# Rows of x and first value weights moved from a hand-written order into the planner's streams, with square sums of the first outputs ranked last

## Chip, cores and metric

The kernel runs on one core of one Trainium2 chip. The metric is the device time of one execution in microseconds (us). The engines are named as in the profile: PE is TensorE, ACT ScalarE, DVE VectorE, POOL GpSimd, SP SyncE, which issues every DMA.

## Reference

One layer of a streaming encoder with 1024 rows of 1024 float32 values. What concerns the change is its beginning and the end of its attention:

```python
h = rmsnorm(x, g_mix_pre)
proj = h @ w_in                   # fq fk fv f_logit cq ck cv
y_fox = forgetting_attention(fq, fk, fv, f_logit)         # 8 heads of 64, causal
y_chk = chunked_relpos_attention(cq, ck, cv, rel_bias)    # 8 heads of 64, 9 chunks
y = concat(rmsnorm(y_fox, g_fox_out), rmsnorm(y_chk, g_chk_out))
x = x + rmsnorm(y @ w_out, g_mix_post)
```

Then follow a cross-attention into 256 memory tokens (`w_mq`, `w_mk`, `w_mv`, `w_mo`) and a squared-ReLU MLP with 4096 hidden values, each with its norms and its residual.

## The kernel before

**Products.** Every float32 product is made of three matmuls (`mm3`, L191 to L195). Each operand is split into a rounded copy, hi, made by ACT, and a difference, lo, made by DVE or POOL as operand minus hi; hi x hi, hi x lo and lo x hi are summed in a PSUM bank. So nothing can be multiplied before ACT has written its hi and DVE or POOL its lo. The PSUM has two banks under each of four names, `mm`, `s`, `tr` and `pv`.

**First part, written out by hand** (L1345 to L1397). The 1024 rows of x are eight blocks x0 to x7 of 128 rows. For each block, `load_x` (L263) issues the load, `norm_x` (L269) takes the sum of squares on ACT (L208), the inverse root on POOL in two operations on 128x1 (L202, L203) and the scaling by root and gain, `gpre`, on DVE (L272). `to_T` (L211) turns two blocks at a time with 16 PE transposes (L218) into the `tr` and `s` banks; ACT copies each bank to `hT_hi` (L231) and DVE subtracts for `hT_lo` (L232). `gpre` is the gain spread over 128 partitions by a PE product with ones, copied by DVE (L1356). Two blocks of weights give values for four heads each: `w_v1` in two pieces (four chunks of 128 rows each), `w_v0` in three (three, three and two chunks, with eight gate columns). `value_weights` (L290) loads a piece, `value_split` (L302) and `split_w` (L181) split it: hi on ACT (L187), lo on DVE or POOL (L188). `values` (L311) makes 24 matmuls for one block of rows and one weight, then an ACT copy (L319) and a DVE difference (L322) into the value tile, and a small ACT copy of the gate columns (L321). The order is fixed by a loop over pairs of blocks: values of `w_v1` for the pair, then the transposes of the next pair, then values of `w_v0` for the pair. Three buffers (`wraw`) hold raw weight pieces; a load into one waits until the piece before it has been split. SP issues its DMAs in program order, so what stands behind such a load waits too.

**Attention, ordered by a planner.** `Flow` (L56) is a model run while the kernel is built. Streams (generators such as `score_steps`, `turn_steps`, `value_steps`, `filler_steps`) yield one PE step each with a cost and a condition. The first stream in the list whose condition holds gives the next PE step. Work for ACT, DVE, POOL and SP is put into queues with the time from which it can start, a cost and a rank (`level`); of the work that is due, the lowest rank goes first. `Tokens` count free buffers and banks; `seen` holds when something will be there. The result is a fixed order on each engine; on the chip the engines wait for each other by semaphores. `Stock` (L346) holds the list of weight blocks in the order of loading, splits them and gives the buffers back; `home` names the kind of buffer that each block is split into. `Outputs` (L941) loads the attention outputs back in two head groups and two halves of the rows, and puts the split, the squares and their sum in the queues; `rstd_steps` (L995) sums the squares over partitions on PE. Scores are taken in pieces of two matmuls (L593), reduced by DVE with their bias (L597); probabilities are turned by PE (`ptr`, L671), split by ACT and DVE (`ph` L680, `pl` L677) and multiplied with the values (`pv`, L708 and L709).

Two `flow.run` calls share the work: one for attention, which also makes keys and values of the memory tokens (`mk`, `mv`) as filler, and one for the output projection (`w_out`, tiles `yw`) and the cross-attention. The planner's clock starts at zero where attention starts: it takes all engines for free then. Past the cross-attention, the order is written out by hand again.

## Time and profile before

| what | value |
|---|---|
| median of 3 runs | 1498.51 us (1498.42 to 1498.52) |
| the profiled execution | 1498.03 us |
| its span, first to last instruction | 1496.2 us |
| granted TensorE clock | 0.999 |
| PE busy | 1474.1 us (99%) |
| DVE, ACT, POOL busy | 936.3, 790.3, 402.1 us |

How to read it: the page gives the busy time of each engine, and views of the trace give busy time in stages, the waits of an engine with the instruction that ended them, and single instructions in order of time: start, length, engine, line, operation, out<-in, shape, and in brackets the idle time before it and its releaser. "L188" is a line of the kernel before. A row with "x2" stands for two instructions in a row; rows that summarise give minimum, median and maximum in ns. Records of PE overlap, since matmuls are pipelined: the distance between two starts is what one costs.

### The profile page before, as it was taken

The page shows a single profiled execution, that of the slowest core. Times are in us where ns is not written, and L with a number is a line of the kernel's source. Part 1 is how long each engine was busy: PE and PEld are TensorE (multiplying, and loading weights), DVE is VectorE, ACT ScalarE, POOL GpSimd, SP SyncE. Part 2 cuts the span into 40 slices and gives each one's busy share as a digit, 9 for nine tenths or more (in the row PEclk, how much of TensorE's full clock was granted, in tenths as well). Part 3 has the DMA queues.
Part 4 walks back from the last instruction along what each step waited for, and adds up shares of the span by engine and source line. Part 5 has one row for each costly group of instructions (what it writes and reads, how often), then busy time and mean ns, then how long its engine had stood idle before and what let it go on. Part 6 is the DMA issues. An engine that isn't in the chain of part 4 may idle for free.

```text
span 1496.2 us, 21615 instructions
## 1 busy us (share of the span) xinstructions
PE 1474.1 (99%) x7628; PEld 1253.2 (84%) x7628; DVE 936.3 (63%) x1617; ACT 790.3 (53%) x1405; POOL 402.1 (27%) x629
## 2 busy tenths in 40 slices
PE   8999999999999999999999999999999999999998
PEld 7989888888889888888888887888888888888886
DVE  5377677565576834884375577675555675646577
ACT  5367576575666835554354455555555553444442
POOL 4244355353354300521031423333333000000021
PEclk9999999999999999999999999999999999999999
DMA  4223312512224552461241355774445695436475
GB/s 170 90 74 88 84 40 92 152 53 64 75 67 149 175 176 85 141 211 57 85 169 57 115 180 192 263 244 149 149 151 176 225 346 203 141 120 215 173 252 197
DMA packets 82766, 218.58 MB, mean 146 GB/s; under 512 B 9801, under 2 KB 13905, under 8 KB 82658
## 3 DMA queue, kind: packets, MB, share of 16 engines
q1 hardware_dynamic: 82658, 217.20, 43.7%
q8 instruction: 60, 0.98, 0.3%
q14 instruction: 48, 0.39, 0.1%
HBM read 157.86 MB, written 50.91 MB: 140 GB/s over the span
## 4 chain that ended last, share of the span: by engine, by line
PE 92%; DVE 3%; DMA 1%; POOL 1%; ACT 1%; issue 1%; SPq 0%; DVEq 0%; POOLq 0%; ACTq 0%
PE ptr L671 4%; PE fx L194 4%; PE fx L195 4%; PE fx L193 4%; PE fy L194 3%; PE fy L195 3%; PE fy L193 3%; PE px L195 3%; PE px L194 3%; PE px L193 3%; PE pv L709 2%; PE pv L708 2%; PE k L193 2%; PE k L195 2%; PE k L194 2%; PE pz L193 2%
## 5 line engine op out<-in xcount | busy, mean ns | idle before, releaser
L677 DVE TENSOR_TENSOR pl<-ptr,ph 128x512 fp32r<-128x512 f32 (+1 forms) x152 | 92.2, 615 | 39.7 <-ACT ph L680 33.9
L1788 ACT ACTIVATE whif<-ra 128x1024 fp32r<-128x1024 f32 x37 | 39.2, 1060 | 122.0 <-PE fy L194 62.6
L1790 DVE TENSOR_TENSOR wlof<-ra,whif 128x1024 fp32r<-128x1024 f32 x37 | 45.3, 1224 | 91.1 <-ACT whif L1788 91.1
L680 ACT ACTIVATE ph<-ptr 128x512 fp32r<-128x512 f32 (+1 forms) x152 | 79.2, 539 | 39.2 <-PE ptr L671 32.6
L1904 POOL TENSOR_SCALAR rf<-sf 128x1 f32<-128x1 f32 x8 | 8.2, 1027 | 326.5 <-ACT jf L1889 326.2
L709 PE MATMUL pv<-pl,vs 128*128 128x256 f32 x304 | 78.8, 283 | 1.9 <-DVE pl L677 1.9
L708 PE MATMUL pv<-ph,vs 128*128 128x256 f32 x304 | 79.8, 286 | 0.0
L194 PE MATMUL fx<-vlof,whif 128*128 128x512 f32 x168 | 65.4, 389 | 0.0
L193 PE MATMUL fx<-vhif,whif 128*128 128x512 f32 x168 | 65.4, 389 | 0.0
L195 PE MATMUL fx<-vhif,wlof 128*128 128x512 f32 x168 | 65.4, 389 | 0.0
L709 PEld LDWEIGHTS pv<-pl,vs 128*128 128x128 f32 x304 | 57.6, 189 | 6.7 <-DVE pl L677 1.5
L708 PEld LDWEIGHTS pv<-ph,vs 128*128 128x128 f32 x304 | 57.3, 189 | 4.0
L1678 POOL TENSOR_TENSOR sc<-wf,wf 128x512 f32<-128x512 f32 x14 | 22.0, 1568 | 142.9 <-DMA wf<-in_w_ff 142.9
L193 PE MATMUL k<-hT_hi,whik 128*128 128x512 f32 x128 | 52.7, 412 | 0.0
L193 PE MATMUL mq<-h2T_hi,whimq 128*128 128x512 f32 x128 | 52.1, 407 | 0.0
L193 PE MATMUL q<-hT_hi,whiq 128*128 128x512 f32 x128 | 50.9, 398 | 0.0
L194 PE MATMUL yw<-wlowo,yT_hi 128*128 128x512 f32 x128 | 49.9, 390 | 0.5 <-DVE wlowo L410 0.5
L193 PE MATMUL ym<-whimo,oT_hi 128*128 128x512 f32 x128 | 50.3, 394 | 0.1
L193 PE MATMUL yw<-whiwo,yT_hi 128*128 128x512 f32 x128 | 50.3, 393 | 0.0
L195 PE MATMUL k<-hT_hi,wlok 128*128 128x512 f32 x128 | 50.3, 393 | 0.0
L195 PE MATMUL mq<-h2T_hi,wlomq 128*128 128x512 f32 x128 | 50.1, 392 | 0.0
L195 PE MATMUL q<-hT_hi,wloq 128*128 128x512 f32 x128 | 50.1, 391 | 0.0
(596 smaller groups left out, 5026.1 us busy)
## 6 DMA issues: line engine op xcount, KB each, us to landing
ra<-gd SPq DMA_DIRECT2D x56, 512.0 KB, 4.0
wg<-in_w_ff SPq DMA_DIRECT2D x56, 512.0 KB, 6.0
wf<-in_w_ff SPq DMA_DIRECT2D x38, 512.0 KB, 4.0
gd<-s SPq DMA_DIRECT2D x48, 256.0 KB, 2.1
wrawmq<-in_w_mq SPq DMA_DIRECT2D x16, 512.0 KB, 4.0
wrawmo<-in_w_mo SPq DMA_DIRECT2D x16, 512.0 KB, 3.8
gd<-u SPq DMA_DIRECT2D x32, 256.0 KB, 2.1
gd<-g SPq DMA_DIRECT2D x25, 256.0 KB, 2.5
```

The costliest lines, as they stand in the source:

```text
L193: nc.tensor.matmul(ps, lh, rh, start=start, stop=False, skip_group_check=more)
L194: nc.tensor.matmul(ps, lh, rl, start=False, stop=False, skip_group_check=more)
L195: nc.tensor.matmul(ps, ll, rh, start=False, stop=stop, skip_group_check=more)
L671: nc.tensor.transpose(tr[:, m, :], sp[:, k * P:(k + 1) * P], ident)
L677: flow.put("V", at, 0.7, lambda: nc.vector.tensor_sub(pl[:, live, :], tr[:, live, :], f(ph[:, live, :])), done)
L680: flow.put("S", flow.end, 0.6, lambda ph=ph, tr=tr, live=live: nc.scalar.activation(ph[:, live, :], tr[:, live, :], AF.Copy), split)
L708: nc.tensor.matmul(pv, v, ph[:, hs, :], start=c == 0 and half == 0, stop=False)
L709: nc.tensor.matmul(pv, v, pl[:, hs, :], start=False, stop=c + 1 == len(steps) and half == 1)
L1678: eng.tensor_sub(sc[:, k1], r0[:, k0], r1[:, k0])
L1788: nc.scalar.activation(ah, ra, AF.Copy)
L1790: nc.vector.tensor_sub(al, ra, f(ah))
L1904: nc.gpsimd.tensor_scalar(r, ssf[b][:, 0:1], ssf[b][:, 1:2], EPS, op0=ALU.add, op1=ALU.add)
```

## The change

The hand-written first part is taken out. Loads of x and of the two first value weights become entries of `Stock`'s list (`u1` for `w_v1`, `u0` for `w_v0`), in the order x0, first piece of u1, x1, second piece of u1, x2, first piece of u0, x3, x4, x5, the other two pieces of u0, x6, x7. Two new streams, `x_turn_steps` and `first_value_steps` (once for u1, once for u0), stand ahead of the others in the attention's list, and the planner's clock starts with the first load. x0 and x1 are loaded and squared in two halves of 512 columns; every block is scaled in two halves. x0 to x3 are turned one block at a time, x4 to x7 in pairs. The lo of each piece of u1 is made in halves, one on DVE and one on POOL at the same time; the lo of all pieces of u0 is made by POOL. u1 is split into the `w` buffers as before, u0 into `u4` buffers, both by the planner; the load of the bias row, its reversal and its store (`bias_rows`) become a pump. Scores may begin only once the gates have taken their buffers (`"gating"`). A third piece of `w_mv`'s first half goes to a `u4` buffer. In `Outputs`, all work of the first head group (copies, differences, squares and their sums) gets rank 3, where it had 1. `rstd_steps` for the second half of the first group and the pump of `Outputs` go to the second `flow.run`. The number of matmuls and transposes, and their shapes, stay the same.

```diff
-            dict(s=2, tr=2, pv=2, mm=2, sp=1, p=2, klo=4, bias=2, raw=2, w=0, u4=6,
+            dict(s=2, tr=2, pv=2, mm=2, sp=0, p=2, klo=1, bias=2, raw=3, w=2, u4=6,
...
-            self.blocks = []
+            u = {k: (k, t["w_v0" if k[0] == "u0" else "w_v1"][:, a:b, :], [P, b - a, 264 if k[0] == "u0" else 256])
+                 for k, a, b in ((("u1", 0), 0, 4), (("u1", 1), 4, 8),
+                                 (("u0", 0), 0, 3), (("u0", 1), 3, 6), (("u0", 2), 6, 8))}
+            self.blocks = ["x0", u["u1", 0], "x1", u["u1", 1], "x2", u["u0", 0], "x3", "x4", "x5",
+                           u["u0", 1], u["u0", 2], "x6", "x7", "small"]
+            self.bus = 0.5
...
-            self.home.update({("mv", nh, kp): "u4" for nh in range(2) for kp in (1, 3)})
+            self.home.update({("mv", *k): "u4" for k in ((0, 1), (0, 2), (0, 3), (1, 1), (1, 3))})
             turn = 0
+            self.home.update({("u0", i): "u4" for i in range(3)})
...
+        def moved(self, key, share=1.0):
+
+            def landed(at):
+                self.bus = max(self.bus, at + 1.5) + 1.75 * share
+                seen[key] = self.bus + 0.2
+            flow.put("D", flow.now, 0.42, lambda: None, landed)
...
+                if key[0] == "u1":
+                    both = all_of(key, 2, free["raw"].give)
+
+                    def apart(at, key=key, both=both):
+                        for half, (eng, e, cost) in enumerate((("V", nc.vector, 0.69), ("G", nc.gpsimd, 1.3))):
+                            done = all_of((key, half), 1, both)
+                            flow.put(eng, at, cost, lambda half=half, e=e: self.lo(key, e, half), done)
+
+                    flow.put("S", flow.now, 1.06, lambda key=key: self.hi(key), apart)
+                    continue
+                vec = key[0] not in ("q", "k", "v", "u0") and (key[0] != "mk" or key[1] % 2)
...
+                    if key[0] == "u0":
+                        flow.put(eng, at, 2.1, lambda: self.lo(key, e), last)
...
-                               lambda: there(("qk", n), ("bias", n, a)) and free["s"].ready()
+                               lambda: there(("qk", n), ("bias", n, a), "gating") and free["s"].ready()
...
+            lv = 3 if g == 0 else 1
...
-                flow.chain(at, [("V", 0.7, call) for call in adds], done, 1)
+                flow.chain(at, [("V", 0.7, call) for call in adds], done, lv)
...
-                                dst, o, AF.Square), squared, 1)), 1)
+                                dst, o, AF.Square), squared, lv)), lv)
...
-    def rstd_steps(g):
-
-        for th in range(2):
+    def rstd_steps(g, ths=(0, 1)):
+
+        for th in ths:
...
+    def x_load(b):
+        tag = "sp" if b % 3 else "klo"
+        x = xrow[b] = p1.tile([P, D], F32, tag=tag, bufs=5 if b % 3 else 4, name=f"x_{b}")
+        cols = [slice(0, HT), slice(HT, D)] if b < 2 else [slice(0, D)]
+        r, ss = (small.tile([P, k], F32, tag=m, bufs=8, name=f"{m}_x{b}") for m, k in (("rstd", 1), ("ssx", 2)))
+        def root():
+            if b > 1:
+                nc.gpsimd.tensor_scalar(r, ss[:, 0:1], EPS, None, op0=ALU.add)
+            else:
+                nc.gpsimd.tensor_scalar(r, ss[:, 0:1], ss[:, 1:2], EPS, op0=ALU.add, op1=ALU.add)
+            nc.gpsimd.tensor_tensor(r, r, mhalf[:, 0:1], op=ALU.pow)
+        def scale(h):
+            c = slice(h * HT, (h + 1) * HT)
+            nc.vector.scalar_tensor_tensor(x[:, c], x[:, c], r, gpre[:, c], op0=ALU.mult, op1=ALU.mult)
+        def rooted(at):
+            lv = min(b // 2, 2)
+            flow.put("G", at, 0.95, root, lambda at: flow.chain(at, [("V", 0.7, lambda: scale(0))], lambda at: (
+                mark(("xn", b, 0))(at), flow.put("V", at, 0.7, lambda: scale(1), mark(("xn", b, 1)), lv)), lv))
+        summed = all_of(("ssx", b), len(cols), rooted)
+        for i, c in enumerate(cols):
+            nc.sync.dma_start(x[:, c], t["x"][b * P:(b + 1) * P, c])
+            def square(i=i, c=c):
+                junk = p1.tile([P, D], BF16, tag="ph", bufs=2, name=f"junk{b}{i}")
+                nc.scalar.activation(junk[:, c], x[:, c], AF.Square, scale=1.0 / 32.0, accum_out=ss[:, i:i + 1])
+            def landed(at, square=square):
+                stock.bus = max(stock.bus, at + 1.5) + 1.75 / len(cols)
+                flow.put("S", stock.bus + 0.2, 0.17 + 0.9 / len(cols), square, summed, min(b // 2, 1))
+            flow.put("D", flow.now, 0.42, lambda: None, landed)
...
+    def x_turn_steps():
+        for bs in ((0,), (1,), (2,), (3,), (4, 5), (6, 7)):
+            n = len(bs)
+            act, c0 = hT[bs[0] // 4], bs[0] % 4 * P
+            per = 4 // n
+            for k in range(0, KC, per):
+                bank = ("tr", "s")[k // 4]
+                yield 0.436, lambda: there(*(("xn", b, k // 4) for b in bs)) and free[bank].ready() and (
+                    bs[0] < 2 or ("first", 1, bs[0] - 2) in seen)
+                free[bank].take()
+                tr = mm_tile([P, per, n, P], f"tr_x{bs[0]}_{k}", bank)
+                for j in range(per):
+                    for q, b in enumerate(bs):
+                        nc.tensor.transpose(tr[:, j, q, :], xrow[b][:, (k + j) * P:(k + j + 1) * P], ident)
+                src = tr.rearrange("p a q b -> p a (q b)")
+                left = all_of(("xt", bs, k), per // 2, free[bank].give)
+                for i in range(k // 2, (k + per) // 2):
+                    part = src[:, 2 * i - k:2 * i - k + 2, :]
+                    dh, dl = act.h[i][:, :, c0:c0 + n * P], act.l[i][:, :, c0:c0 + n * P]
+                    def lo(at, part=part, dh=dh, dl=dl, left=left, i=i, bs=bs, n=n):
+                        def there_now(end):
+                            left(end)
+                            for b in bs:
+                                seen["hT", b, i] = end
+                        flow.put("V", at, 0.16 + 0.26 * n, lambda: nc.vector.tensor_sub(dl, part, f(dh)), there_now)
+                    flow.put("S", flow.end, 0.16 + 0.22 * n, lambda part=part, dh=dh: nc.scalar.activation(
+                        dh, part, AF.Copy), lo)
+            for b in bs:
+                free["sp" if b % 3 else "klo"].give(flow.end)
+    def first_value_steps(g):
+        n = 264 if g == 0 else 256
+        blocks = ((0, 3), (3, 6), (6, 8)) if g == 0 else ((0, 4), (4, 8))
+        where = [(i, kc - a) for i, (a, b) in enumerate(blocks) for kc in range(a, b)]
+        def split(at):
+            for pair in (2, 3) if g == 0 else (0, 1):
+                for th in range(2):
+                    seen["v", pair, th] = at
+        done = all_of(("first", g), TB, split)
+        logits = all_of("fcol", TB) if g == 0 else None
+        for kb in range(TB):
+            cs = slice((kb % 4) * P, (kb % 4 + 1) * P)
+            for kc in range(KC):
+                i, j = where[kc]
+                w = ("u0", i) if g == 0 else (("u1", i), j // 2)
+                yield 3 * (n / 2400 + 0.0135), lambda: there(w, ("hT", kb, kc // 2)) and (kc or free["mm"].ready())
+                if kc == 0:
+                    free["mm"].take()
+                    ps = mm_tile([P, n], f"v{g}_{kb}")
+                wh, wl = stock.w[f"u{g}", i]
+                mm3(ps, hT[kb // 4].hi(kc, cs), hT[kb // 4].lo(kc, cs), wh[:, j, :], wl[:, j, :], kc == 0, kc == KC - 1)
+            seen["first", g, kb] = flow.end
+            src = ps[:, 0:256].rearrange("p (h d) -> p h d", d=64)
+            v = vs[g][kb // 2][:, kb % 2, :, :]
+            def lo(at, src=src, v=v):
+                flow.put("V", at, 0.43, lambda: nc.vector.tensor_sub(v[:, :, 64:128], src, f(v[:, :, 0:64])),
+                         lambda end: (free["mm"].give(end), done(end)))
+            def hi(src=src, v=v, ps=ps, kb=kb):
+                nc.scalar.activation(v[:, :, 0:64], src, AF.Copy)
+                if g == 0:
+                    nc.scalar.activation(fcol[:, kb, :], ps[:, 256:264], AF.Copy)
+            flow.put("S", flow.end, 0.38 + 0.1 * (g == 0), hi, lambda at, lo=lo: (logits and logits(at), lo(at)))
+        for i in range(len(blocks)):
+            stock.done((f"u{g}", i))
...
-                seen["v", n, th] = 0.0
-        biases = Biases()
-        flow.pumps += [stock.pump, biases.pump, outputs.pump]
-        flow.run([value_steps(), turn_steps(), score_steps(), side_steps(), rstd_steps(0),
-                  filler_steps(keep)])
+        flow.pumps += [stock.pump, biases.pump, outputs.pump, bias_rows]
+        flow.run([x_turn_steps(), first_value_steps(1), first_value_steps(0), value_steps(), turn_steps(),
+                  score_steps(), side_steps(), rstd_steps(0, (0,)), filler_steps(keep)])
         return keep
 
-    stock = Stock()
+    stock, biases = Stock(), Biases()
+    others = {"norm": (3, mem_norm), "mem": (2, mem_loads), "small": (0, small_loads)}
+    others.update({f"x{b}": (0, lambda b=b: x_load(b)) for b in range(TB)})
...
-        xs = [load_x(0), load_x(1)]
-        raw1 = value_weights(1)
-        xs += [load_x(2), load_x(3)]
...
-        w1 = value_split(1, raw1[0], 0, nc.vector)
-        w1 += value_split(1, raw1[1], 1, nc.gpsimd)
-        to_T(xs[0], xs[1], hT[0], 0, "x0", ("tr", "s"))
-        raw0 = []
-        value_weights(0, raw0, 0)
-        xs += [load_x(4), load_x(5)]
-        value_weights(0, raw0, 1)
-        value_weights(0, raw0, 2)
-        w0 = []
-        for b in range(0, TB, 2):
-            if b + 2 < TB:
-                for i in (b + 2, b + 3):
-                    norm_x(xs[i], i)
-            if b == 0:
-                w0 += value_split(0, raw0[0], 0, nc.vector)
-            values(1, w1, vs[1], b)
-            if b == 0:
-                w0 += value_split(0, raw0[1], 1, nc.gpsimd)
-            values(1, w1, vs[1], b + 1)
-            if b == 0:
-                w0 += value_split(0, raw0[2], 2, nc.gpsimd)
-            if b + 2 < TB:
-                to_T(xs[b + 2], xs[b + 3], hT[(b + 2) // 4], (b // 2 + 1) % 2 * 256, f"x{b + 2}", ("tr", "s"))
-            if b == 0:
-                xs += [load_x(6), load_x(7)]
...
-            if b == 6:
-                stock.split_now(2)
-            for kb in (b, b + 1):
-                values(0, w0, vs[0], kb)
+
+        vs = {g: [u4(f"vs{g}_{i}", (P, 2, 4, P)) for i in range(4)] for g in (1, 0)}
...
-        flow.pumps[1] = Rows().pump
-        flow.run([memory_out_steps(), memory_turn_steps(), memory_score_steps(), rstd_steps(1), second_rows(),
+        flow.pumps[1:] = [Rows().pump, outputs.pump]
+        flow.run([memory_out_steps(), memory_turn_steps(), memory_score_steps(), rstd_steps(0, (1,)), rstd_steps(1), second_rows(),
...
```

164 lines of the change are left out of this document (38 added, 126 removed).

## Prediction

> **What bounds the kernel now.** I read the page first, then busy time by stage, then what TensorE (PE) waited for.
>
> ```profile
> span 1496.2 us, 21615 instructions
> PE 1474.1 (99%) x7628; PEld 1253.2 (84%) x7628; DVE 936.3 (63%) x1617; ACT 790.3 (53%) x1405; POOL 402.1 (27%) x629
> ```
>
> PE is busy for 1474.1 of 1496.2 us, so all idle time together is 22.1 us (1.5%). In the two built programs PE issues the same 7612 matmuls and transposes of the same shapes. The change can therefore only move PE's idle time. Where is it? The first fence is busy time by stage (first number the length, second PE's), the second PE's waits over the whole span (total, times, longest).
>
> ```profile
> 12.17:21.66 9.49, 8.24 (x67) 8.00 (x65) 7.75 (x9) 7.92 (x16) 8.28 (x7) 1.00 0.76 297
> 21.66:65.71 44.05, 44.05 (x368) 44.05 (x369) 18.72 (x33) 15.83 (x39) 10.17 (x13) 1.00 0.13 41
> 100.00:160.00 60.00, 60.00 (x388) 54.15 (x385) 46.22 (x150) 45.27 (x102) 30.29 (x74) 1.00 0.25 68
> 510.00:520.00 10.00, 8.10 (x49) 6.75 (x49) 9.84 (x17) 9.72 (x20) 0.70 (x4) 1.00 0.49 168
> ```
>
> ```profile
> PE tr_x L218 <- DVE x L272: 2.5, 1, 2.5
> PE pv L709 <- DVE pl L677: 1.9, 4, 0.9
> PE v L193 <- DVE vs L322: 1.3, 1, 1.3
> PE yw L194 <- DVE wlowo L410: 0.5, 1, 0.5
> ```
>
> From 21.66 to 65.71, where the first query matmul starts, PE never stops; it does not stop from 100 to 160 either. What the change touches is the start, up to 21.66, and the end of attention at 510 to 520 (1.9 us of waits for the differences pl, 0.5 for a split of w_out). The other waits lie past 550, where PE's order is the same in both programs, so I leave them.
>
> Busy time overstates PE at the start, because a record stretches while PE waits. I count issue distance instead.
>
> ```profile
> 13.34 0.28 PE L195 MATMUL v<-whiv,hT_lo 128*128 128x256 f32 x1
> 13.46 0.28 PE L193 MATMUL v<-whiv,hT_hi 128*128 128x256 f32 x1
> 21.66 0.39 PE L193 MATMUL v<-whiv,hT_hi 128*128 128x264 f32 x1 [1.25 <-DVE vs L322]
> 33.48 1.75 PE tr_x L218 x16
> ```
>
> A value matmul costs 0.12 us (13.34 to 13.46), a transpose 1.75/16 = 0.109. By 21.66 PE had issued 48 value matmuls and 32 transposes: 5.8 + 3.5 = 9.3 us of work, so **12.4 us are idle at the start**. That is the number the change must beat.
>
> **The start.** Removed is the hand-written order; now x and the first value weights are streams of the planner. Half rows are loaded, squared and scaled for x0 and x1; the first weight block is issued ahead of x1; x0 to x3 are turned singly, between value matmuls. Here are the rows that price the steps.
>
> ```profile
> 5.00 1.06 ACT L208 ACTIVATE junk<-x 128x1024 bf16<-128x1024 f32 x1 [3.00 <-DMA x<-in_x]
> 5.96 0.19 ACT L208 ACTIVATION_READ_ACCUMULATOR junk<-x 128x1 f32 x1
> 6.05 0.69 DVE L1356 COPY gpre<-gpre 128x512 f32<-128x512 f32 x1 [1.02 <-PE gpre L1355]
> 6.24 0.23 POOL L202 TENSOR_SCALAR rstd_x<-ss_x 128x1 f32<-128x1 f32 x1 [4.95 <-ACT junk L208]
> 6.55 0.57 POOL L203 TENSOR_TENSOR rstd_x<-rstd_x,mhalf 128x1 f32<-128x1 f32 x1
> 7.15 1.28 DVE L272 SCALAR_TENSOR_TENSOR x<-x,rstd_x,gpre 128x1024 f32<-128x1024 f32 x1 [0.41 <-POOL rstd_x L203]
> 8.36 1.06 ACT L187 ACTIVATE whiv<-wrawv 128x1024 fp32r<-128x1024 f32 x1 [0.96 <-DMA wrawv<-in_w_v]
> 8.49 4.02 PE L218 MATMUL tr_x<-ident,x 128*128 128x128 f32 x16 [2.48 <-DVE x L272]
> 10.41 1.22 DVE L188 TENSOR_TENSOR wlov<-wrawv,whiv 128x1024 fp32r<-128x1024 f32 x1
> 10.78 3.08 POOL L188 TENSOR_TENSOR wlov<-wrawv,whiv 128x1024 fp32r<-128x1024 f32 x1 [1.61 <-ACT whiv L187]
> 17.67 4.77 POOL L188 TENSOR_TENSOR wlov<-wrawv,whiv 128x792 fp32r<-128x792 f32 x2 [0.29 <-ACT whiv L187]
> 18.62 2.65 DVE L188 TENSOR_TENSOR wlov<-wrawv,whiv 128x792 fp32r<-128x792 f32 x1
> 24.86 0.38 ACT L319 ACTIVATE vs<-v 128x256 fp32r<-128x256 f32 x1 [3.01 <-PE v L195]
> 25.34 0.42 DVE L322 TENSOR_TENSOR vs<-v,vs 128x256 fp32r<-128x256 f32 x1 [1.02 <-ACT fcol L321]
> L413 POOL TENSOR_TENSOR wlov<-wrawv,whiv x8: 1288/1290/1298, 225.8 to 413.0; 128x512 fp32r<-128x512 f32 x8
> 5.00:10.00 5.00, 2.52 (x9) 1.51 (x8) 2.80 (x4) 3.71 (x6) 2.40 (x4) 1.00 1.01 336
> ```
>
> The rows at 10.41, 17.67 and 18.62 matter most. DVE's difference of 1024 columns took 1.22, so 792 should take 0.95; beside POOL's differences it took 2.65, ending at 21.27. POOL's difference of 512 columns takes 1.29 alone, so 792 and 528 take about 3.3; they took 4.77. And POOL's 1024 took 3.08 where two halves make 2.6. So a DVE operation with two SBUF operands (the splits, and the scaling of x with gpre) and a POOL operation do not run together. I read it as a lock: the one that comes second waits for the other's whole instruction.
>
> The Trainium skill, "SBUF — State Buffer", section "Who interferes with whom", says just that of a VectorE instruction with two SBUF inputs and a GpSimd one that reads SBUF: who issues first has the port pair for the whole instruction. If the rows meant sharing instead, each meeting would cost some 0.7 us rather than 1.3 to 1.95, the first term below would be about -1 and the sum about -2. The rule speaks against this change, which puts all of u0's differences on POOL.
>
> The chain, step by step (all its times are estimates from these rows, in the order of the built program). The halves of x0 are squared by 5.7, the root takes 0.9, the gpre copy ends at 6.74; so x0's halves are scaled (1.28/2, say 0.7 each) by 7.45 and 8.1, and the first transpose starts at 7.5 (8.49 now). The weight block is behind 0.5 MB less, at 336 GB/s 1.5 us earlier: its hi half starts at about 6.9 and ends at 8.0. POOL's half of the lo asks at 8.05, while DVE is scaling: POOL gets 8.1 to 9.4, DVE's half follows, to 10.05. Then the hT_lo of 256 columns (about 0.4 each) and 12 matmuls, to 11.7. By now x1's root is done (10.7), but POOL's half of the second block (its hi ends at 11.3) comes in ahead of x1's scaling: 13.4, then DVE's half of that block and a POOL root, x1's second half at 15.5; v0 ends at 16.75. POOL's 792 columns of u0 (1.95) start at 15.7 and hold x2's scaling until 17.65; x2 is scaled at 18.35 and 19.05, v1 ends at 21.35. x3's square stands on ACT behind the copies of x2's transposes; its root is there at 22.55, its scaling at 23.9, just when v2's first 21 matmuls are through. v3 needs the bank of v2, whose lo stands on DVE behind the scalings of x4: 27.2. From there I find no wait. PE has then issued 81 value matmuls and 32 transposes, 13.2 us: idle 14.0, **+1.6 against now**. If DVE comes first at 8.05, the chain ends at 27.0; I take **+1.5**. Bounds: without any meeting the same chain reaches v3 at 22.1, idle 8.9, -3.5; with POOL ahead of the scalings of x5 and x7 as well (1.95 and 1.3), +4.8. I take the value near the row of 2.65, which shows a meeting.
>
> ```profile
> 11.65 2.57 SPq L298 DMA_DIRECT2D wrawv<-in_w_v  x2
> 65.71 0.39 PE L193 MATMUL q<-hT_hi,whiq 128*128 128x512 f32 x1
> 66.17 0.39 PE L195 MATMUL q<-hT_hi,wloq 128*128 128x512 f32 x1
> ```
>
> SP: the second and third blocks of u0 wait for the splits of u1 (at about 10 and 14.3; between 11.65 and 14.2 now), and x6, x7 behind them; they land by about 18 and are squared after 25, so this is free. The loads of the first query weights and of the bias row go out tens of us earlier; they stand behind nothing urgent, and their first reader is the matmul at 65.71 or later. Free.
>
> **The first scores.** Their order changes until about 160 us, with longer runs: eight score matmuls in a row where there were two or four.
>
> ```profile
> 499.39 0.55 DVE L597 CUSTOM_DVE_ANT_0 spc7g<-sc7g,biasc 128x384 f32<-128x384 f32 x1
> ```
>
> A piece (two matmuls, about 0.3 us) is emptied by DVE in 0.55, with two banks: in a run of four pieces the last two wait some 0.25 each. PE stops nowhere from 100 to 160 now, so this can only lose: **+0.4**, from 0 to 1.2.
>
> **The end of attention.** The squares of the outputs get the last rank on ACT and DVE (the first group's copies and differences too), one more w_mv block goes to buffers that are free earlier, and w_out's loads are issued before the outputs of the second half.
>
> ```profile
> 513.38 0.75 DVE L986 SCALAR_TENSOR_TENSOR yT_lo<-oin,gcol,yT_hi 128x512 fp32r<-128x512 f32 x1
> 514.91 0.39 PE L709 MATMUL pv<-pl,vs 128*128 128x256 f32 x1 [0.90 <-DVE pl L677]
> 539.22 2.01 ACT L404 ACTIVATE whiwo<-wrawwo 128x1024 fp32r<-128x1024 f32 x2 [1.22 <-DMA wrawwo<-in_w_out]
> L410 DVE TENSOR_TENSOR wlomv<-wrawmv,whimv x8: 1206/1222/1227, 491.5 to 531.1; 128x1024 fp32r<-128x1024 f32 x8
> ```
>
> Now a 0.75 us output operation stands ahead of pl, and PE waits 0.90. In the changed order w_mv matmuls lie between the last pv groups, so three of the four waits are covered. One place is left: four output differences (3.0) and a w_mv split (1.2) before the last pl (0.55), 4.8 us on DVE, under 18 w_mv matmuls of 0.23 (half of 65.71 to 66.17), 4.1: 0.7 to 0.9 of waiting. So -1.0; the 0.5 for w_out goes too, as its load is issued earlier: **-1.5**, from -2.4 to +0.5 (if DVE reaches that place late). The sum for the second half of the outputs moves behind 24 w_out matmuls (5.5 us) and needs some 4 after the last w_mv matmul: nothing.
>
> **Sum.** +1.5 + 0.4 - 1.5 = +0.4 us. The profiled execution took 1498.03 us (span 1496.2 and 1.8 around it), 0.48 below the median of the runs, 1498.51; the sum is the same on either, so I forecast 1498.9 as a median: **no change**.
>
> **Rivals.**
> 1. *The meetings do not happen* (DVE comes first, or its scaling is not held): the start gives -3.5, the sum is -3.5 + 0.4 - 1.5 = -4.6: 1493.9. For it: the scalings took 1.28 each time now, never longer. Against it: the 2.65 row, and POOL, which has more to do beside them than now. 0.2.
> 2. *POOL's u0 differences hold the scalings of x5 and x7 too*, so that PE has no product left: it decides from the point where x5 is scaled later than about 29 us. Start +4.8, sum +3.7: 1502.2. For it: ACT and DVE have 10 and 16 more instructions there. Against it: in the chain x5's root is there at 25.5 and its scaling is not needed before 29. 0.13.
> 3. *It changes nothing where it says*: a start as long as now and the end of attention still waiting for pl: 1498.5, within the forecast's band.
>
> **How the numbers follow.** About 0.2% (3.0 us) is what a measurement of this kernel can tell from no change. Forecast and third rival: 0.67 within it; first rival 0.20 faster; second 0.13 slower. The range reaches to near both: 1494.2 to 1502.0, leaving out about 0.08 below and 0.07 above.
>
> **What would show it.** First transpose near 7.5; the first query matmul at 67.2 (+1.5 on 65.71); scalings of x1 or x2 that start when a POOL difference ends; waits of pv for pl under 1 us in all. A query matmul at or before 63 would make the first term wrong, one after 68.5 the second rival right; a wait of over 1 us among the first scores, or pv waiting 2 us again, would break the other two terms.

## The result and the profile after

Seven executions of the changed kernel took 1500.58 to 1504.04 us, median **1501.53**, beside 1498.42 for the kernel before: a ratio of 1.0025, 95% interval 1.0013 to 1.0036. It is slower by about 3 us. The forecast was 1498.9. The profiled execution took 1501.05 us, and its span is 3.1 us longer than before. In the fence, first lines of the page after: PE is still busy for almost all of it.

```profile
span 1499.3 us, 21676 instructions
PE 1476.1 (98%) x7628; PEld 1254.1 (84%) x7628; DVE 939.4 (63%) x1633; ACT 790.3 (53%) x1417; POOL 400.9 (27%) x631
```

Where did the 3.1 us come from? PE issues the same matmuls, so I compare when it issues the same ones. The rows of the query products and of the transposes `tr_h2T` give the first and the last start of each group, before and then after.

```profile
L193 PE MATMUL q<-hT_hi,whiq x128: 387/390/478, 65.7 to 425.7; 128*128 128x512 f32 x128
L1150 PE MATMUL tr_h2T<-ident,yw x64: 270/272/330, 614.4 to 668.3; 128*128 128x128 f32 x64
```

```profile
L174 PE MATMUL q<-hT_hi,whiq x128: 387/389/478, 69.3 to 430.5; 128*128 128x512 f32 x128
L1059 PE MATMUL tr_h2T<-ident,yw x64: 270/272/328, 617.0 to 670.9; 128*128 128x128 f32 x64
```

The lag is 3.6 us at the first query matmul, 4.8 at the last (430.5 against 425.7) and 2.6 at the first `tr_h2T` (617.0 against 614.4); the span is 3.1 longer. So the **start lost 3.6** (forecast 1.5), the stretch of the **first scores lost 1.2** (forecast 0.4), and the **end of attention gained 2.1** (forecast 1.5); 0.5 comes later, at px, where PE waits 1.7 for `wlo_a` instead of 1.2. These lags are read from one execution of each kernel; experiment 3 has a second look at the start of the kernel before.

Busy time by stage after. The start is longer: PE now stops in each of these three stretches up to 69.31.

```profile
11.37:17.12 5.75, 5.49 (x23) 4.97 (x23) 5.10 (x9) 4.76 (x11) 4.96 (x7) 1.00 0.94 373
17.12:22.00 4.88, 4.51 (x40) 4.34 (x39) 4.88 (x9) 2.72 (x8) 1.75 (x1) 1.00 1.01 340
22.00:69.31 47.31, 45.89 (x384) 45.47 (x383) 20.80 (x41) 18.97 (x47) 14.89 (x20) 1.00 0.21 66
```

PE's waits after: 2.5 for x is now 1.4, but 1.7 for `hT_hi` is new; the 1.3 for a value bank (`vs`) is now 1.4, in two other places; of the 1.9 us for `pl` 0.4 is left, beside 0.4 for `ph`; the wait for `wlowo` is gone.

```profile
PE v L174 <- ACT hT_hi L1334: 1.7, 1, 1.7
...
PE tr_x L1320 <- DVE x L1260: 1.4, 1, 1.4
PE v L174 <- DVE vs L1369: 1.4, 2, 1.0
...
PE sc0g L500 <- DVE mnc0g L504: 0.4, 1, 0.4
PE pv L616 <- DVE pl L584: 0.4, 1, 0.4
PE pv L615 <- ACT ph L587: 0.4, 1, 0.4
```

Three places of the start, from the timelines of the changed kernel. First, ACT stood 4.19 us for the first weight block and began its hi at 9.38, so PE's first product came at 11.37:

```profile
9.38 1.06 ACT L295 ACTIVATE whiu<-wrawu 128x1024 fp32r<-128x1024 f32 x1 [4.19 <-DMA wrawu<-in_w_v]
```

```profile
7.69 1.97 PE L1320 MATMUL tr_x<-ident,x 128*128 128x128 f32 x8 [1.45 <-DVE x L1260]
11.37 0.58 PE L174 MATMUL v<-whiu,hT_hi 128*128 128x256 f32 x1 [1.71 <-ACT hT_hi L1334]
...
12.69 0.41 PE L175 MATMUL v<-wlou,hT_hi 128*128 128x256 f32 x1
12.90 0.41 PE L176 MATMUL v<-whiu,hT_lo 128*128 128x256 f32 x1
...
35.67 0.38 PE L174 MATMUL v<-whiu,hT_hi 128*128 128x256 f32 x1 [0.97 <-DVE vs L1369]
```

Second, DVE operations with two SBUF operands stretch where POOL works on weights. Compare each DVE row with the POOL row at its time:

```profile
14.11 1.76 DVE L304 TENSOR_TENSOR wlou<-wrawu,whiu 128x512 fp32r<-128x512 f32 x1
17.13 2.96 DVE L1260 SCALAR_TENSOR_TENSOR x<-x,rstd_x,gpre 128x512 f32<-128x512 f32 x2
26.91 0.74 DVE L1332 TENSOR_TENSOR hT_lo<-tr_x,hT_hi 128x256 fp32r<-128x256 f32 x2
30.42 2.47 DVE L1260 SCALAR_TENSOR_TENSOR x<-x,rstd_x,gpre 128x512 f32<-128x512 f32 x2 [0.26 <-POOL rstd_x L1256]
```

```profile
13.77 1.56 POOL L304 TENSOR_TENSOR wlou<-wrawu,whiu 128x512 fp32r<-128x512 f32 x1 [0.42 <-ACT whiu L295]
16.98 1.89 POOL L301 TENSOR_TENSOR wlou<-wrawu,whiu 128x792 fp32r<-128x792 f32 x1
26.72 2.02 POOL L301 TENSOR_TENSOR wlou<-wrawu,whiu 128x792 fp32r<-128x792 f32 x1
30.36 1.31 POOL L301 TENSOR_TENSOR wlou<-wrawu,whiu 128x528 fp32r<-128x528 f32 x1
```

Two scalings of 512 columns take 1.41 elsewhere (at 6.89); those of x2 took 2.96 and those of x6 2.47. `hT_lo`, whose one operand is in PSUM, runs at its usual length beside POOL (26.91). Third, the wait of 0.97 at 35.67: x6's scaling (at 30.42), held until 31.7, stands in DVE's queue ahead of the four `hT_lo` of x4 and x5 and of the value difference of `v3`, which frees a bank for `v4`.

The value matmuls at 12.69 and 12.90 stand 0.21 apart, where before (13.34 to 13.46) they cost 0.12; they reach 0.12 at 17.7. The clock column reads 1.00 there, but the clock's records begin only at 17.05, and the distance says that PE ran at about half rate. This was the first suspect.

### The profile page after: what moved, and what is told of

Its sections match the earlier page's. It is cut to its first block, busy times and chain, and to the rows that moved or that the text cites. A ratio compares the mean times of both kernels' runs of the same rounds, so it can differ in the third digit from the quotient of the medians.

```text
span 1499.3 us, 21676 instructions
## 1 busy us (share of the span) xinstructions
PE 1476.1 (98%) x7628; PEld 1254.1 (84%) x7628; DVE 939.4 (63%) x1633; ACT 790.3 (53%) x1417; POOL 400.9 (27%) x631
## 4 chain that ended last, share of the span: by engine, by line
PE 91%; DVE 3%; DMA 2%; ACT 2%; POOL 1%; issue 1%; SPq 0%; DVEq 0%; POOLq 0%; ACTq 0%
PE ptr L578 4%; PE fx L175 4%; PE fx L176 4%; PE fx L174 4%; PE fy L176 3%; PE fy L175 3%; PE fy L174 3%; PE px L176 3%; PE px L174 3%; PE px L175 3%; PE pv L616 2%; PE pv L615 2%; PE k L174 2%; PE yw L174 2%; PE k L176 2%; PE k L175 2%
## 5 line engine op out<-in xcount | busy, mean ns | idle before, releaser
L175 PE MATMUL k<-hT_lo,whik 128*128 128x512 f32 x128 | 50.1, 391 | 0.0
L175 PE MATMUL q<-hT_lo,whiq 128*128 128x512 f32 x128 | 50.1, 391 | 0.0
```

Of the source, the lines that this page charges most:

```text
L175: nc.tensor.matmul(ps, lh, rl, start=False, stop=False, skip_group_check=more)
```

## The experiments

**Theory at the start:** the half-rate clock makes some 2.0 of the 3.6 us, since the changed kernel's PE stops between its first transposes and its first product. **Rival:** inputs bound the start, above all those that POOL holds; PE at full rate would only wait. The kernel before ran beside each group of kernels (medians 1499.41 to 1499.81 there), and each ratio below is to those runs.

**1. Idle transposes (e1_warm)**, eight behind the gpre products and eight ahead of the first value product.
```diff
+        for i in range(8):
+            nc.tensor.transpose(idle[:, i % 4, :], ident, ident)
...
+                if (g, kb, kc) == (1, 0, 0):
+                    for q in range(8):
+                        nc.tensor.transpose(idle[:, q % 4, :], ident, ident)
```


> The changed kernel with 16 idle transposes of the identity on PE, whose results nobody reads: eight behind the gpre products, eight ahead of the first value product, so that PE does not rest there. Theory (half-rate clock): in the changed kernel a value matmul cost 0.21 us instead of 0.12 until 17.1 us, against 13.2 us before, which is about 2.0 of the 3.6 us that the first query matmul moved (65.71 to 69.31). With PE kept busy, value matmuls cost 0.12 from about 12 us on, the first query matmul comes at about 67.3 and the time is about 1499.5. Rival (inputs): PE would have waited for x1's scaling and the second weight block's difference (ends 15.87) anyway; the matmuls get quick but the waits for inputs grow by as much: first query matmul at 68.8 or later, time 1501.0 to 1501.5.

Ratio 1.0020 (1.0010 to 1.0030), first query matmul at 69.7. Value matmuls cost 0.12 from 11.7 on, and PE was 1.2 us ahead of the changed kernel at 13.5; then it waited for inputs. The rows are its stops between 12 and 16.5:

```profile
13.66 0.66 PE L1320 MATMUL tr_x<-ident,x 128*128 128x128 f32 x4 [0.70 <-DVE x L1260]
15.34 0.39 PE L175 MATMUL v<-wlou,hT_hi 128*128 128x256 f32 x1 [0.90 <-DVE wlou L304]
```

What the theory forecast did not come. But this run alone does not refute it: its clock column falls back to 0.50 from 15.9 to 19.3, and value matmuls stand 0.21 apart there again. The control in experiment 4 decides.

**2. No weight difference on POOL (e2_dve).**
```diff
-    enumerate((("V", nc.vector, 0.69), ("G", nc.gpsimd, 1.3))):
+    enumerate((("V", nc.vector, 0.69), ("V", nc.vector, 0.69))):
-    vec = key[0] not in ("q", "k", "v", "u0") and (...)
+    vec = key[0] not in ("q", "k", "v") and (...)
...
-                        flow.put(eng, at, 2.1, lambda: self.lo(key, e), last)
+                        flow.put(eng, at, 0.95, lambda: self.lo(key, e), last)
```


> The changed kernel with all differences of u1 and u0 on DVE, none on POOL, so that no POOL operation of any length meets the scalings of x. Rival (inputs, held by POOL): in the changed kernel a DVE difference took 1.1 us more than alone at 14.11, the scalings of x2 1.5 more at 17.13 and those of x7 1.1 more at 30.42; with them gone the first query matmul comes 1.5 to 2.5 us earlier, at 67 to 68, and the time is 1499 to 1500. Theory (half-rate clock): DVE gets as much work back (1.35 + 2.6 us of differences) as it loses in holds, and the clock still rises near 17: first query matmul at 68.8 to 69.3, time 1501.0 to 1501.5.

Ratio 1.0000 (0.9991 to 1.0009), first query matmul at 66.6. The rival holds: with POOL out of the way the start is 2.7 us shorter. (The scaling at 30.42, which the expectation gives to x7, is that of x6.) One thing goes along with the edit: the planner reckons with other costs, so its order changes too, on PE from the 17.12 of the changed kernel on. The same is true of every edit below that moves differences or loads, so a first query matmul shows edit and order together.

**3. The end of attention by itself (e3_end_alone), and taken out (e4_no_end).** The first puts rank 3, the third `w_mv` block in `u4` and the split `rstd_steps` into the kernel before; the second undoes them in the changed one.
```diff
-            lv = 3 if g == 0 else 1
+            lv = 1
...
-            self.home.update({("mv", *k): "u4" for k in ((0, 1), (0, 2), (0, 3), (1, 1), (1, 3))})
+            self.home.update({("mv", nh, kp): "u4" for nh in range(2) for kp in (1, 3)})
...
-    rstd_steps(0, (0,)), filler_steps(keep)])
+    rstd_steps(0), filler_steps(keep)])
...
```


> The kernel before with the end-of-attention part alone: rank 3 for the first group's output work, the third w_mv block in a u4 buffer, the second half's sum of squares in the second run. Theory: the lag of the changed kernel fell from 4.7 us (at 497) to 2.6 (at 570), so this part is worth -2.1 us by itself: 1496.3. Rival: the gain hung on the other order or the later arrival of PE in the changed kernel; alone it gives under 0.5: 1498.0 to 1498.4.

> The changed kernel with the end-of-attention part undone (rank 1, w_mv as before, both halves of the sum of squares in the first run). Theory: the 2.1 us are lost again and pv waits near 1.9 us for pl: 1503.6. Rival: the gain hung on the new order of the first part: 1501.5 to 1502.

Taken out, the ratio is 1.0054 (1.0041 to 1.0066): the waits come back (`pl` 2.3, `wlowo` 0.6), and a half-rate stretch with them (last section). One of its five executions, at a granted clock of 0.998, took 1503.70, as expected; the other four, at 0.996, took 1506.99 to 1507.46. But alone, in the kernel before, it is a loss: 1.0026 (1.0016 to 1.0036). Its waits in the profile of that kernel:

```profile
PE pv L709 <- DVE pl L677: 2.8, 4, 1.5
...
PE yw L193 <- ACT whiwo L404: 1.0, 1, 1.0
PE yw L194 <- DVE wlowo L410: 0.8, 1, 0.8
```

There are two half-rate stretches as well (clock 0.50 from 517 to 520.2 and from 547.5 to 550.9), worth 3.4 us. So the ranks as such do not bring the 2.1 us, and my expectation was wrong here. That the part gains together with the order that the planner finds after the new start is argued from these two runs, not shown.

This profile holds a third thing, which the part did not cause. Its start is the unchanged one, instruction for instruction, yet its first query matmul came at 66.7, where the profile of the kernel before has 65.7. A scaling of x, 1.28 otherwise, took 2.95, because POOL's weight difference began 0.02 us ahead of it; in the profile before, the scaling began at 17.42 and POOL's difference, at 17.67, came second. DVE and POOL here:

```profile
17.32 2.95 DVE L272 SCALAR_TENSOR_TENSOR x<-x,rstd_x,gpre 128x1024 f32<-128x1024 f32 x1 [0.77 <-POOL rstd_x L203]
```

```profile
17.30 1.89 POOL L188 TENSOR_TENSOR wlov<-wrawv,whiv 128x792 fp32r<-128x792 f32 x1
```

So the kernel before has such a meeting too, and a few tenths of a microsecond decide who is held: its first query matmul came at 65.7 in one profile and at 66.7 in the other, and the loss of 3.6 is 2.6 beside the second.

**4. Which of POOL's differences.** The changed kernel once more as a control, then only u0 or only u1 on DVE, then u0's first block or the later two alone.

> The changed kernel once more, beside the next three on one chip. If the half-rate clock windows are what spreads its times, a second trace shows the clock reach full at another moment than 17.1 us, and the first query matmul moves with it by more than 0.5 us from 69.31; if inputs bound the start, the first query matmul stays at 68.8 to 69.8 whatever the clock does. Ratio to the kernel before about 1.0025 on either.

> The changed kernel with the differences of u0 on DVE and those of u1 in halves on DVE and POOL as changed. Theory now (POOL operations hold the scalings of x): if the holds by u0 (1.5 us at 17.13, 1.1 at 30.42) are the cause, most of the gain of the kernel with no weight difference on POOL comes back: first query matmul at 66.6 to 67.6, ratio 1.0000 to 1.0008. Rival (u1's POOL halves are the cause): first query matmul at 68.5 or later, ratio 1.0018 to 1.0025.

> The changed kernel with both halves of u1's differences on DVE and those of u0 on POOL as changed. If u1's POOL halves are the cause (DVE's half took 1.76 instead of 0.69 at 14.11, and PE waited for it until 15.93): first query matmul at 66.6 to 67.6, ratio 1.0000 to 1.0008. If u0's are: 68.5 or later, ratio 1.0018 to 1.0025.

The edit for u0 is the second and third change of experiment 2, that for u1 the first. For u0's first block alone it is the following; for the later two it has `key[1] > 0`. In both, the cost of a block that goes to DVE is 0.95, as in experiment 2.
```diff
+    vec = (key[1] == 0 if key[0] == "u0" else key[0] not in ("q", "k", "v")) and (...)
```


> The changed kernel with the difference of u0's first block alone on DVE; the second and third stay on POOL. With all three on DVE the first query matmul came at 66.36 instead of 69.3. If the hold of x2's scaling (1.5 us at 17.13, the meeting that the prediction's chain had) is most of it: first query matmul at 66.4 to 67.4. Rival (the later blocks hold x5 to x7, the prediction's second rival): 68.0 to 69.0, and PE still waits near 28 and 35 for a value bank.

> The mirror: u0's first block on POOL as changed, the second and third on DVE. If x2's hold is most of it: first query matmul at 68.2 to 69.3. If the later blocks' holds are: 66.4 to 67.6. If the two add up, each of the two kernels stands about 1.5 us from 69.3 and together they give 2.9.

| kernel | first query matmul | ratio (95% interval) |
|---|---|---|
| the changed one again | 69.3 | 1.0017 (1.0008 to 1.0026) |
| u0 on DVE | 66.4 | 1.0000 (0.9991 to 1.0009) |
| u1 on DVE | 67.1 | 1.0015 (1.0006 to 1.0024) |
| u0's first block on DVE | 69.6 | 1.0021 (1.0012 to 1.0030) |
| u0's later blocks on DVE | 69.2 | 1.0014 (1.0005 to 1.0023) |

The control also settles the clock for the changed kernel: its matmuls were at 0.12 from 16.2 on, 1.5 us earlier than in the first profile; then PE stood idle 0.79 instead of 0.37 ahead of x2's transposes, which came at 19.5 in both, and its first query matmul came at the same time. u0 on DVE gives back 2.9 us, but each half of that edit alone gives nothing. With the first block on DVE, x2 is scaled in time (1.40 instead of 2.96), and PE is 1.3 us ahead at 24.6, up to where its order is the changed kernel's; 0.3 of that is an earlier weight block. Then POOL's second block meets the scaling of x5, and one hold takes the place of another. DVE, POOL and PE there:

```profile
25.21 2.36 DVE L1260 SCALAR_TENSOR_TENSOR x<-x,rstd_x,gpre 128x512 f32<-128x512 f32 x1 [0.46 <-POOL rstd_x L1256]
```

```profile
25.15 1.88 POOL L301 TENSOR_TENSOR wlou<-wrawu,whiu 128x792 fp32r<-128x792 f32 x1
```

```profile
27.63 0.55 PE L1320 MATMUL tr_x<-ident,x 128*128 128x128 f32 x3 [1.27 <-DVE x L1260]
```

A wait of 1.42 for a value bank follows at 35.99. With the later blocks alone on DVE no scaling behind x2's is held any more; yet PE's lead of 0.4 at 29.8 is down to 0.1 by the first query matmul, over two waits for value banks (0.46 and 0.57), in another order. What causes these was not told apart.

What u1's halves bring stays open: the profiled execution of that kernel was the shortest of its 11 (1498.81, median 1501.83), so its trace is not the usual one. The granted clock was 0.999 in the three shortest and 0.996 to 0.998 in the other eight, so half-rate stretches may have taken what the start gave.

**5. Whole rows (e11_whole with u0 on DVE, e12_whole_only without).**
```diff
-        cols = [slice(0, HT), slice(HT, D)] if b < 2 else [slice(0, D)]
+        cols = [slice(0, D)]
...
-            if b > 1:
+            if len(cols) == 1:
```


> u0's differences on DVE, and x0 and x1 loaded and squared whole, not in halves (packets of 4 KB instead of 2 KB). The prediction had the first weight block split from 6.9 us on; it came at 9.38, 8.40 and near 9 in the runs so far. If small packets slow the loads (246 GB/s from 2.5 to 5 us where the kernel before moved 349): the hi of the first weight block starts at 7.9 or earlier, and the first transpose at about 8.3. Rival (the loads in flight share the queues, so that a block lands when about 2 MB have landed in all, as in the kernel before): it starts at 8.2 to 9.4 as before, the first transpose is late for nothing, and the first query matmul comes at 66.4 to 67.5.

> The changed kernel with x0 and x1 loaded and squared whole; POOL's differences stay as changed. With u0 on DVE as well, the first weight block's hi started at 7.11 (9.38 in the changed kernel) and the first query matmul came at 65.56. If the late weight block is a cause of its own: the hi starts near 7.1 here too, PE starts its products by 10.2, and the first query matmul comes at 67 to 68.3, ratio 1.0005 to 1.0015. Rival (POOL's holds take back whatever is early): hi near 7.1, but the first query matmul at 68.8 to 69.4, ratio 1.0018 to 1.0025.

Alone: hi of the first weight block at 7.05, first query matmul at 67.0, ratio 1.0005 (0.9996 to 1.0013). With u0 on DVE: 65.6, just ahead of the kernel before (65.7), ratio 0.9993 (0.9985 to 1.0002). ACT's row and the loads from 2.5 to 7.5 us in the kernel with whole rows alone (GB/s is the last number):

```profile
7.05 1.06 ACT L295 ACTIVATE whiu<-wrawu 128x1024 fp32r<-128x1024 f32 x1 [0.94 <-DMA wrawu<-in_w_v]
```

```profile
2.50:5.00 2.50, 2.50 (x3) 0.95 (x4) 0.59 (x1) 0.04 (x1) 0.00 (x0) 1.00 0.85 287
5.00:7.50 2.50, 1.07 (x2) 0.00 (x0) 1.18 (x3) 1.56 (x3) 0.80 (x2) 1.00 0.97 311
```

and in the changed kernel:

```profile
2.50:5.00 2.50, 2.50 (x3) 1.13 (x4) 0.42 (x1) 1.16 (x3) 0.00 (x0) 1.00 0.93 246
5.00:7.50 2.50, 1.25 (x2) 0.00 (x0) 1.48 (x3) 0.19 (x2) 0.87 (x2) 1.00 0.84 243
```

So the halves are a second cause of their own, worth 2.3 us alone (with the order that the planner makes of them); both edits together give 3.7, less than 2.3 + 2.9. The hi of that block began at 8.40 to 9.40 in the 13 profiles with halves and at 7.05 to 7.22 in the five with whole rows. Whole rows have packets of twice the size and also one DMA less ahead of the weight block, so that SP issues its load earlier. First the changed kernel, then the one with whole rows:

```profile
2.01 0.43 SPq L282 DMA_DIRECT2D wrawu<-in_w_v  x1
```

```profile
1.54 0.41 SPq L282 DMA_DIRECT2D wrawu<-in_w_v  x1
```

The packets speak against their size: up to 9 us in the changed kernel, those of 2048 bytes took 84 ns and those of 4096 bytes 159 (medians), about the same for a byte. No run tried the two apart.

**6. Idle transposes once the inputs are early, and the place near 907.** The start's idle transposes are those of experiment 1, the other edits those of 2 and 5. Near 907 the edit is this one (`j == 3` and eight transposes in e14 and e15, which came ahead of another product, at 893.7).
```diff
         x = bank(f"px{j}", tags[0])
+        if j == 5:
+            for q in range(9):
+                nc.tensor.transpose(x[:, 0:P], ident, ident)
```

> No weight difference of u1 and u0 on POOL, and the 16 idle transposes as well. Without them that kernel had the clock full only at 16.6 us, and its value matmuls from 10.39 to 16.5 cost 0.21. If inputs no longer bound the start, the clock does: with PE busy from 6 us on, the first query matmul comes 1 to 2 us earlier than at 66.57, and the ratio to the kernel before is 0.9985 to 0.9993. If inputs still bound it (x1's scalings end at 15.0): under 0.4 us earlier, ratio 0.9998 to 1.0002.

> u0's differences on DVE, u1's in halves on both engines, and the 16 idle transposes. If the clock binds once no POOL operation holds a scaling: ratio to the kernel before 0.9985 to 0.9995, first query matmul at 65.4 to 66.0. If it does not: as without them, ratio 1.0000, first query matmul at 66.2 to 66.5.

> x0 and x1 whole, u0's differences on DVE, and the 16 idle transposes: what the runs so far point to. If with early inputs the clock is the bound: first query matmul at 64.4 to 65.2 and ratio 0.9980 to 0.9990. If not: 65.4 to 65.8, ratio 0.9990 to 0.9996, as without the idle transposes.

> The changed kernel with eight idle transposes at one place far from the change: ahead of the px product for which PE waits 1.2 and 0.5 us near 907. Theory (windows): several traces show the clock at half for 3.41 us just behind that place, the rest do not, and the times of one kernel lie in two groups 1.7 us apart (1501.1 to 1501.5 and 1502.9 to 1504.0). With PE busy in that wait no window falls, and all runs lie near the lower group: median 1501.1 to 1501.5, spread under 1 us. Rival (the spread comes from elsewhere, DMA say): the spread stays 2 to 3 us and the median 1502.

> x0 and x1 whole, u0's differences on DVE, and the eight idle transposes near 907 without those at the start. If both hold: as the kernel with the first two (1498.3, spread 1496.6 to 1501.1) without its upper group, median 1496.8 to 1497.3, ratio 0.9980 to 0.9987. If the spread comes from elsewhere: ratio 0.9993 as without them.

> The changed kernel with nine idle transposes at the px product of 907.8 itself; in the earlier try they came before another px product, at 893.7, and the wait of 1.2 us at 907 stayed as it was. Theory (windows): PE no longer rests 2 us within 3.4 there, no half-rate window follows near 909, and all runs lie in the lower group: median 1501.0 to 1501.5, spread under 1.2 us. Rival (the spread comes from elsewhere): median 1502, spread 2 to 3 us.

> x0 and x1 whole, u0's differences on DVE, the 16 idle transposes at the start and the nine at 907.8. As the kernel without the last nine (first query matmul at 65.0, median 1498.6, spread 1.2), less the upper group's share if windows make the groups: median 1497.2 to 1498.0, ratio 0.998 to 0.999. If they don't: 1498.6, ratio 0.9993.

| kernel | first query matmul | ratio (95% interval) |
|---|---|---|
| no POOL, idle transposes (e7) | 66.1 | 0.9989 (0.9980 to 0.9998) |
| u0 on DVE, idle transposes (e10) | 67.8 | 1.0000 (0.9991 to 1.0009) |
| whole rows, u0 on DVE, idle transposes (e13) | 65.0 | 0.9993 (0.9984 to 1.0002) |
| changed, idle at 893.7 (e14) | 69.7 | 1.0016 (1.0007 to 1.0025) |
| whole rows, u0 on DVE, idle at 893.7 (e15) | 65.1 | 0.9994 (0.9985 to 1.0003) |
| changed, idle at 907.8 (e16) | 69.3 | 1.0011 (1.0002 to 1.0020) |
| e13 with idle at 907.8 (e17) | 65.1 | 0.9995 (0.9986 to 1.0004) |

The expectation of e13 (0.9980 to 0.9990) was too good, and so were those of e15 and e17: 0.5 us earlier at the start did not show in the ratio. That of e10 missed the other way: 67.8 is 1.4 later than without idle transposes. Its clock fell back to 0.50 from 16.0 to 19.5, as in e1, and from x2's transposes on PE is 1.4 us behind, in the same order. So with early inputs a half-rate stretch at the start does cost time; in e7 and e13, where the clock stayed at 1.00, the first query matmul came 0.4 and 0.5 us earlier than without idle transposes. Only e7 has its interval below 1, by some 1.6 us, of which the start explains 0.4; the others with early inputs are not told apart from the kernel before, or from each other.

## Why the prediction was wrong

**The step that failed is the start's chain**, +1.5 forecast, +3.6 measured, in two of its statements.

"its hi half starts at about 6.9": it started at 9.38. The reckoning had 0.5 MB less ahead of the block, at the rate of the kernel before. Neither came. Two half loads of x0 take two issues, so the block's load was issued at 2.01, no earlier than in the kernel before (2.01); and when its hi began, 1.97 MB had moved (210 GB/s over 9.38 us), where it was 1.93 before (231 over 8.36). From 2.5 us on the rate was 280 GB/s instead of 317. With whole rows the load is issued at 1.54, 1.37 MB had moved (195 over 7.05), and the hi starts at 7.05. By `v3` the lateness had shrunk to 0.8 us: forecast at 27.2, it came at 28.03.

"From there I find no wait": there was 0.97 at 35.67, and with the distance around it 1.1. It is the hold of x6's scaling by u0's third block. 0.83 and 1.13 are 2.0 of the 2.1 us that the term was short. The two are not independent, though. In the profile of e16, whose start is the same program, the hi began 0.5 us earlier (8.88) and so did `v3` (27.49); then x5's scaling met u0's second block (1.92 instead of 1.40), PE's wait grew by as much, and the first query matmul stood at 69.3 again:

```profile
35.65 0.38 PE L174 MATMUL v<-whiu,hT_hi 128*128 128x256 f32 x1 [1.47 <-DVE vs L1369]
```

What held: the meetings of DVE and POOL are exclusive. The chain had POOL's first u0 block hold x2's scalings until 17.65; it held them until 18.87, and they took 2.96. The Trainium skill, "SBUF — State Buffer", section "Who interferes with whom", calls the port pair that the two engines share an exclusive lock, and says that a VectorE instruction with at most one SBUF input, outside its two-port modes, does not contend; the rows of `hT_lo` (0.74 at 26.91), whose other input is in PSUM, agree. So the first rival (no meetings, 1493.9) fell. Its argument, that the scalings took 1.28 each time in the kernel before, held for that one profile: in experiment 3 one took 2.95.

**The second rival** named what came: u0's differences hold later scalings as well. It had 0.13, priced at 1502.2; the time was 1501.53. Its price was 3.3 us over the forecast, and the hold that did come cost 1.1; the rest was the late weight block, which no rival had. Its test, a first query matmul after 68.5, came true (69.31). The argument against it ("in the chain x5's root is there at 25.5 and its scaling is not needed before 29") looked at one block, while the hold came at x6; DVE's rows follow each other in one order, and the held scaling stood ahead of five differences that PE needed.

**First scores:** +1.2, the upper bound of the term. The wait that the profile shows, 0.4 at 108.7, is of the kind forecast (a run of score pieces, two banks), with DVE standing at an output copy that waits for ACT. The other 0.8 is in no wait that the view lists. No run changed this alone, so the cause is read from the trace only.

**End of attention:** -2.1 against -1.5, inside its bounds, by the waits named; taken out, they came back. That it is no gain alone was not foreseen.

The forecast's sum was thus short by 2.1 (start) and 0.8 (scores), less 0.6 (end of attention) and with 0.5 later at px, a stretch that it had left out because PE's order is the same there: 0.4 became 3.1. The range held the time, at its upper end.

## What to carry to other kernels

Before work is put on an engine because it is free there, look which operations of its neighbour it excludes, and follow the neighbour's whole queue behind the one that is held: removing one such meeting moved the next scaling into another. An earlier place in the list of loads is only worth what the loads ahead of it leave: with the first rows in halves the block behind them was there about 2 us later than with whole rows. And a part that gains in one order of a planner can lose in another, so it has to be tried in the order in which it will stand.

## What the runs showed of the hardware

Times of one kernel spread over 2 to 5 us, and the traces show two reasons. One is who comes first where DVE and POOL meet (1.0 us in experiment 3). The other is single stretches of 3.4 us at half clock, in the middle of the kernel. Busy time by stage of the changed kernel run again, and then of the one with idle transposes at 907.8 (PEclk is the third number from the right):

```profile
906.00:909.30 3.30, 1.62 (x7) 0.73 (x5) 1.60 (x3) 3.12 (x5) 0.00 (x0) 0.99 0.00 0
909.30:912.60 3.30, 3.30 (x8) 2.63 (x9) 2.18 (x3) 0.02 (x1) 0.00 (x0) 0.50 0.49 169
```

```profile
906.00:909.30 3.30, 2.59 (x16) 1.74 (x15) 1.64 (x2) 3.01 (x4) 0.00 (x0) 1.00 0.00 0
909.30:912.60 3.30, 3.30 (x16) 2.73 (x15) 1.92 (x3) 0.60 (x1) 0.00 (x0) 1.00 0.63 197
```

PE had been idle for 1.7 of 3.3 us, and then issued 8 matmuls where 16 go otherwise: 1.7 us lost. The first profile of the changed kernel has the same waits there and no such stretch. With PE kept busy in that wait (e16), 11 runs lay between 1500.76 and 1501.97, where the 11 of the control, on another chip, lay between 1501.07 and 1503.22. It is no cure: e17, with the same idle transposes at 907.8, lay between 1497.55 and 1501.66, and the longest of these, which was profiled, has its half-rate stretch from 893.9 to 897.3, behind a wait of 1.87 us. The Trainium skill, "TensorE: Matmul & The Clock Gate", section "What's actually happening", has PE's clock judged over free-running windows of 3.4 us; the length agrees, and so does that the same wait counts or not by where the window falls. It asks for a whole idle window, though, and here half of one was enough. In the kernel without the part for the end of attention such a stretch followed its waits for `pl`, from 521.6 to 525, and a second came near 914 to 917.6, so taking the part out cost more than its waits.

A meeting of DVE and POOL is not confined to DVE operations with two SBUF inputs: with u0's first block on DVE (e8), a `TENSOR_SCALAR` of 8x256, with one, took 1.39 us instead of 0.27, beside a POOL difference from 31.61 to 32.92.
